# Modulation vectors moved between stages of a two-layer hybrid flow step

## The chip, the cores and the metric

The kernel runs on one core of a Trainium2 chip. The metric is the device time of one execution in microseconds; three runs of the kernel before gave 3373.78, 3359.71 and 3369.78 us, so the median is 3369.78 us. Engines are named as the profile names them: PE is TensorE, DVE VectorE, ACT ScalarE, POOL GpSimd; SP only issues transfers, and all transfers of this kernel go through its one queue, in order.

## The reference, cut to what matters

1152 tokens (1024 of a 64-column grid and 128 of context) of 1024 features pass two layers. In each layer six modulation vectors come from a conditioning vector, one set for the grid's condition and one for the context's:

```python
def ada_modulation(cond, w_mod, b_mod):
    m = (jax.nn.silu(cond) @ w_mod + b_mod)[..., None, :]
    return jnp.split(m, 6, axis=-1)

def trunk_layer(x, cond, p, ...):
    sh1, sc1, g1, sh2, sc2, g2 = ada_modulation(cond, p['w_mod'], p['b_mod'])
    h = rms_norm(x, p['norm1']) * (1 + sc1) + sh1
    xa, ga, bq, bff, bfb, bi, bg, cq, ck, cv = jnp.split(h @ p['w_in'], split_points, axis=-1)
    ... # three mixers: A RG-LRU, B HGRN2, C attention
    x = x + g1 * mix
    h2 = rms_norm(x, p['norm2']) * (1 + sc2) + sh2
    x = x + g2 * (jnp.square(jax.nn.relu(h2 @ p['w1'])) @ p['w2'])
```

The first two vectors are wanted at a layer's start, g1 at the output projection, sh2 and sc2 at the norm before the MLP, and g2 only in the MLP's second product.

## The kernel before, in words

Features lie on partitions. A vector of 1024 features is eight tiles of 128, so a layer has 48 modulation tiles, j = 0 to 47: 0 to 7 are sh1, 8 to 15 sc1, 16 to 23 g1, 24 to 31 sh2, 32 to 39 sc2, 40 to 47 g2. `mod_tile` (line 259) makes one tile for both conditions: it loads 128 rows of the transposed `w_mod`, 512 KB, in three pieces of 384, 384 and 256 columns (`wm`), and for each piece and condition runs one multiply-and-sum on VectorE against `sil`, the SiLU of the conditions spread over all partitions (`junk` is the product, `ma` the running sum, line 270). That is three transfers and six such VectorE instructions, each followed by a short read of the accumulator; a scale tile (sc1, sc2) has one more small VectorE instruction (`am`). Here each of the six is called a piece. Under the MLP and the attention the pieces' buffers come from the pool `sq` of four, under the recurrence of mixer A from `g`.

A layer's stages run one after the other, each woven from two or three streams: the recurrence of mixer A (RG-LRU) under projections; the recurrences of mixer B (HGRN2, a tree of levels, `sc` scores) under the other projections; the 36 query tiles of mixer C (`attention`), the first eight under the last projections, the others under the output projection (`wo`); the first product of the MLP, `w1`, and the second, `w2`. The MLP's products are done in blocks by seven products for eight; in the first there are 32 units (`line.add`), each of 84 matmuls, four outputs that VectorE and others take from PSUM (`hr`), and weights split into two parts on ScalarE, GpSimd and VectorE. The two layers run the same code on the same shapes.

Before, layer 0 makes its tiles 0 to 15 at its start, 16 to 47 under the recurrences (ten under A's, 22 under B's; `MODS`, line 457), and all 48 of layer 1 under its own first product, spread in program order over the units 6 to 31 (`MLP_MODS`). Layer 1 makes none; its `sil` is closed after that stage.

The order in which an engine runs its instructions is fixed when the program is built. The framework's scheduler takes the program and orders each engine's list by a simulated timeline; it may put an instruction well ahead of where the program wrote it, if its buffers allow. On the chip each engine, and SP's queue, runs its list strictly in order, waiting where something is not ready.

Of the kernel before, what the change touches and what calls it, by code (L numbers as in the profile page):

```python
# [15 lines left out]
DM = 1024  # L16
KD = DM // P
# [25 lines left out]
# a block of tokens: a quarter of the grid and one of the context  # L43
# [6 lines left out]
MLP_MODS = (6, 32)  # L50
# [9 lines left out]
def weave(main, n_main, side, n_side):  # L60
    """Emits two streams evenly interleaved, by their numbers of steps."""
    done = [0, 0]
    gens = [main, side]
    n = [max(n_main, 1), max(n_side, 1)]
    live = [True, True]
    while live[0] or live[1]:
        i = 0 if live[0] and (not live[1] or done[0] * n[1] <= done[1] * n[0]) else 1
        try:
            next(gens[i])
            done[i] += 1  # L70
        except StopIteration:
            live[i] = False


def weave_steps(main, n_main, side, n_side):
    """The main stream, with the steps of a side stream spread over its own."""
# [10 lines left out]
def weave_at(main, side, counts):  # L87
    """The main stream, with the given number of steps of a side stream after each of its own."""
# [10 lines left out]
def steps(n, span, i):  # L99
    """How many of n steps fall on i when they are spread over a span."""  # L100
# [17 lines left out]
def build(ctx, tc, I, O):  # L118
# [9 lines left out]
    def urgent(gen, offset):  # L128
        """A stream whose instructions go before those around it."""
# [7 lines left out]
    # pools that come and go  # L137
# [20 lines left out]
    def phase(st, tag, bufs, w=NW, side="left"):  # L158
        """A pool of [128, w] tiles for one phase of a layer."""
# [3 lines left out]
    def two_phases(st, tag, n1, n2, w):  # L163
        """The same in two places, by turns n1 and n2 tiles."""
# [66 lines left out]
    def load_cond(c):  # L231
        dma(sil[:, c], I["cond"][c:c + 1].to_broadcast([P, DM]))
        act(sil[:, c], sil[:, c], AF.Silu)
# [3 lines left out]
    # the early columns apart from the others, which come later  # L237
# [18 lines left out]
    # adaLN vectors, feature on partitions: mod[l][:, j, cond]  # L256
# [3 lines left out]
    def mod_tile(l, j, piece):  # L260
        """mod[l][:, j] from the rows of w_mod's transpose, in pieces."""
# [19 lines left out]
    def segs(n):  # L281
        # (lo, hi, cond) within chunk n
# [4 lines left out]
    def rms_sums(xs, n, alone=False):  # L287
        """The sums over the feature tiles of the squares of chunk n."""
# [14 lines left out]
    def rms_scale(sq, ps, w=P):  # L303
        """1/rms of 3w tokens, to be turned."""
# [11 lines left out]
    def rms_turn(R, ps, w=P):  # L316
        """1/rms of 3w tokens on all partitions, in SBUF."""
# [16 lines left out]
    class HT:  # L334
        """Normalised and modulated activations in two float32r parts, [k][n]."""
# [49 lines left out]
    def weight(src):  # L385
        """The float32r parts of a [128, 8, 128] weight tile, as functions of its k."""
# [17 lines left out]
    def project_tokens(l, group, ht, evac, s_):  # L404
        """256 features projected with the tokens on partitions, 128 tokens a step."""
# [16 lines left out]
    def store_mix(t, dst, n, g_):  # L422
        """The float32r parts of a chunk of 128 features of the mixers' output, to DRAM."""
# [7 lines left out]
    class B:  # L431
        """The arrays of one pair of heads, in chunks of 384 tokens."""
# [23 lines left out]
    # where the first layer's later modulation vectors are computed, of 32  # L456
    MODS = (10, 11, 11, 0)
    # the projections under the recurrences of the heads
# [5 lines left out]
    class HGRN:  # L464
        """The recurrence of one pair of heads.

        levels(g): the scores of chunk g's three blocks of 128 tokens, by the levels of a binary tree;
        tail(g): its state updates, and all but the backward states' part of its output;
        back(): the backward states, their part of the output and its norm, in reversed order.
        """  # L470
# [205 lines left out]
    def hgrns(pairs):  # L676
        """Both pairs of heads: the end of each part runs under the levels of the next."""
# [10 lines left out]
    RG_STEPS = 1 + 2 * 7  # L688

    def rglru(l, i, xa, gel, gw, ud, g_):  # L690
# [13 lines left out]
        # each function of ScalarE for both directions at once  # L704
# [53 lines left out]
    def split_q(ps, n, h_t, l_t, sub):  # L758
        # queries in the order (row half, column block, row, column) and scaled
# [20 lines left out]
    def qk_project(l, p, win, ht, qd, kd, s_, ns=range(NCH)):  # L780
# [9 lines left out]
        def evac_k(n, ps):  # L790
            # the grid's rows in pairs, by columns
# [12 lines left out]
    # the grid's upper half for all pairs of heads, then the context's tokens and the lower half  # L804
# [4 lines left out]
    # where the output projection is done, by the tokens' half: of the first features, of the last  # L809
# [3 lines left out]
    def attention(l, qd, kd, vd, pool, out):  # L813
        """All query tiles of the four pairs of heads.

        Yields once the first pair's operands are under way, then after each tile the one that is complete.
        """
# [169 lines left out]
    class Ends:  # L987
        """What becomes of the fifth product and of the four blocks of a product of blocks."""
# [4 lines left out]
    def lo_subs(n):  # L993
        """The engines of a version's seven subtractions, n of them on VectorE."""
        return iter([vsub if (i + 1) * n // 7 > i * n // 7 else psub for i in range(7)])

    class Weights:
        """The left operands of the seven products, version by version, in the order of their use."""
# [56 lines left out]
    class Line:  # L1055
        """Products of blocks one after the other, the end of each under the start of the next."""
# [53 lines left out]
    def pieces(b):  # L1110
        """Block b of tokens by chunks and conditions: (chunk, from, to, condition, place in the block)."""
# [795 lines left out]
```

## Time and profile before

| what | us |
|---|---|
| median of three runs | 3369.78 |
| lowest and highest run | 3359.71, 3373.78 |
| span of the profiled execution | 3359.0 |
| PE busy | 2987.9 (89%) |
| DVE busy | 2627.3 (78%) |
| POOL busy | 1735.7 (52%) |
| ACT busy | 1535.1 (46%) |

The profiled execution has no device time of its own beside its span. The median of the runs is 10.8 us above the span, and the lowest run 0.7 us. The shares are averages over stages with different limits, so the rows below are read stage by stage.

### The profile page before, as it was taken

The numbers are of one execution on the slowest core, as the hardware profiler recorded it, in microseconds if no ns is written. First come the engines' busy times: TensorE is split into PE (matmuls) and PEld (weight loads), VectorE is DVE, ScalarE is ACT, GpSimd is POOL, SyncE is SP. The second block draws the span as 40 slices with busy tenths as digits, with TensorE's granted clock in tenths as the row PEclk, the third lists the DMA queues.
The fourth block names the chain that finished last, engine by engine and source line by source line (L and its number), as shares of the span: only waits on it lengthen the run. The fifth ranks groups of instructions, "written<-read, shape, count | busy, mean of one in ns | idle before, by whom it ended". The sixth has DMA issues, their size and how long they took to land. (4 is left out here: it accounts for less than half of the span.)

```text
span 3359.0 us, 62376 instructions
## 1 busy us (share of the span) xinstructions
PE 2987.9 (89%) x21196; PEld 2829.2 (84%) x21196; DVE 2627.3 (78%) x6417; ACT 1535.1 (46%) x3878; POOL 1735.7 (52%) x1822
## 2 busy tenths in 40 slices
PE   7888998898788888898878899999988999899885
PEld 7877987797788888898878789988878999888885
DVE  7799964678999998999996687345878324899997
ACT  5453234554432225554555533455635333555445
POOL 4541222444744437777765311334546555777776
PEclk8999999999899989999999999999989999999997
DMA  7332449973355555322232212689644333532222
GB/s 269 83 115 89 135 117 272 262 244 114 116 164 159 154 163 171 96 85 89 73 117 67 57 31 78 185 245 289 193 130 122 109 105 106 166 98 86 89 73 73
DMA packets 391070, 452.26 MB, mean 135 GB/s; under 512 B 68192, under 2 KB 293600, under 8 KB 390752
## 3 DMA queue, kind: packets, MB, share of 16 engines
q1 hardware_dynamic: 390752, 448.28, 44.5%
q8 instruction: 168, 2.75, 0.3%
q14 instruction: 150, 1.23, 0.1%
HBM read 339.34 MB, written 108.79 MB: 133 GB/s over the span
## 5 line engine op out<-in xcount | busy, mean ns | idle before, releaser
L184 POOL TENSOR_TENSOR wl<-wr,wh 128x512 fp32r<-128x512 f32 x164 | 226.8, 1388 | 476.6 <-ACT wh L181 380.2
L184 POOL TENSOR_TENSOR ws<-wl,ws 128x512 fp32r<-128x512 f32 x160 | 230.6, 1445 | 231.6 <-ACT ws L181 223.5
L1081 PE MATMUL bB<-t,ws 128*128 128x288 f32 x768 | 240.6, 313 | 73.0 <-DVE hr L193 68.3
L1081 PE MATMUL bB<-T,wt 128*128 128x288 f32 x768 | 240.8, 314 | 67.7 <-ACT bB L181 51.0
L184 POOL TENSOR_TENSOR wt<-wl,wt 128x256 fp32r<-128x256 f32 x296 | 253.0, 862 | 68.7 <-ACT wt L181 65.3
L392 PE MATMUL pj<-hh,wh 128*128 128x384 f32 x640 | 221.5, 351 | 21.4 <-DVE vb L178 7.3
L1082 PE MATMUL bB<-t,ws 128*128 128x288 f32 x768 | 236.3, 308 | 1.0 <-DVE t L187 1.0
L1083 PE MATMUL bB<-t,ws 128*128 128x288 f32 x768 | 236.6, 308 | 0.0
L270 DVE CUSTOM_DVE_ANT_0 junk<-wm,sil,ma 128x384 bf16<-128x384 f32 (+1 forms) x320 | 230.0, 719 | 6.7 <-DMA wm<-in_w_mod 1.9
L1082 PE MATMUL bB<-T,wt 128*128 128x288 f32 x768 | 233.9, 305 | 0.0
L1083 PE MATMUL bB<-T,wt 128*128 128x288 f32 x768 | 232.9, 303 | 0.0
L394 PE MATMUL pj<-hh,wl 128*128 128x384 f32 x640 | 222.4, 348 | 4.2 <-POOL wl L184 4.2
L393 PE MATMUL pj<-hh,wh 128*128 128x384 f32 x640 | 222.9, 349 | 3.4 <-DVE hh L205 3.4
L1081 PEld LDWEIGHTS bB<-t,ws 128*128 128x128 f32 x768 | 153.5, 200 | 81.1 <-DVE hr L193 74.8
L1081 PEld LDWEIGHTS bB<-T,wt 128*128 128x128 f32 x768 | 150.5, 196 | 82.0 <-ACT bB L181 60.6
L184 POOL TENSOR_TENSOR wt<-wr,wt 128x256 fp32r<-128x256 f32 x210 | 184.4, 881 | 60.8 <-ACT wt L181 52.2
L184 POOL TENSOR_TENSOR T<-xb,T 128x288 fp32r<-128x288 f32 x192 | 180.6, 950 | 42.7 <-ACT T L181 42.1
L187 DVE TENSOR_TENSOR xb<-xb 128x288 f32<-128x288 f32 x288 | 190.8, 667 | 11.5 <-POOL B L184 6.3
L181 ACT CAST ws<-wl 128x512 fp32r<-128x512 f32 x160 | 98.7, 620 | 194.8 <-PE bB L1083 91.2
L181 ACT CAST T<-xb 128x288 fp32r<-128x288 f32 x256 | 110.3, 432 | 165.8 <-DVE xb L187 147.3
L1081 PE MATMUL bA<-B,wt 128*128 128x288 f32 x512 | 158.6, 310 | 26.7 <-DVE x L205 23.7
L205 DVE SCALAR_TENSOR_TENSOR x<-bB,mod,x 128x256 f32<-128x256 f32 (+2 forms) x576 | 169.7, 339 | 12.5 <-PE bB L1083 11.5
(336 smaller groups left out, 11474.7 us busy)
## 6 DMA issues: line engine op xcount, KB each, us to landing
wr<-in_w SPq DMA_DIRECT2D x308, 256.0 KB, 3.0
hd<-hr SPq DMA_DIRECT2D x256, 144.0 KB, 2.6
wm<-in_w_mod SPq DMA_DIRECT2D x160, 192.0 KB, 2.7
wr<-in_w_in SPq DMA_DIRECT2D x104, 256.0 KB, 3.1
bi<-in_bias SPq DMA_DIRECT2D x96, 192.0 KB, 4.3
QS<-qd SPq DMA_DIRECT2D x72, 256.0 KB, 4.2
xb<-hd SPq DMA_DIRECT2D x128, 144.0 KB, 2.2
xb<-hd SPq DMA_DIRECT2D x64, 288.0 KB, 2.8
```

The lines of the kernel that those rows point to most:

```text
L181: nc.scalar.copy(out=out, in_=in_)
L184: nc.gpsimd.tensor_tensor(out=out, in0=a, in1=b, op=ALU.subtract)
L187: nc.vector.tensor_tensor(out=out, in0=a, in1=b, op=ALU.subtract)
L205: nc.vector.scalar_tensor_tensor(out=out, in0=a, scalar=s, in1=b, op0=op0, op1=op1)
L270: nc.vector.tensor_tensor_reduce(out=junk[:, :w], in0=r[:, :w], in1=sil[:, c, k0:k0 + w], scale=1.0, scalar=acc[c], op0=ALU.mult, op1=ALU. ...
L392: mm(ps, lhsT=wh(k), rhs=ah(k), start=k == first, stop=False)
L393: mm(ps, lhsT=wh(k), rhs=al(k), start=False, stop=False)
L394: mm(ps, lhsT=wl(k), rhs=ah(k), start=False, stop=k == last)
L1081: mm(ps, lhsT=w[:, 0, ti(i)], rhs=t[:, 0], start=start and i == 0, stop=False, skip_group_check=True)
L1082: mm(ps, lhsT=w[:, 0, ti(i)], rhs=t[:, 1], start=False, stop=False, skip_group_check=True)
L1083: mm(ps, lhsT=w[:, 1, ti(i)], rhs=t[:, 0], start=False, stop=i == n - 1, skip_group_check=True)
```

## The change

The tiles stay the same, 96 in all, and so does what each one costs in instructions. Where they are computed changes:

| stage | before | after |
|---|---|---|
| layer 0, start | 16 | 16 |
| layer 0, recurrences of A and B | 32 | 24 |
| layer 0, first product of the MLP | 48 | 32 |
| layer 1, attention (query tiles 9 to 25) | 0 | 16 |
| layer 1, first product of the MLP | 0 | 8 |

Layer 0's first product now takes the layer's own g2 (40 to 47) and layer 1's 0 to 23. Layer 1's sh2 and sc2 (24 to 39) go under its attention, and its g2 (40 to 47) under its first product. For that `sil` is loaded and activated once more in layer 1, in memory that was kept empty as a pad.

```diff
-MLP_MODS = (6, 32)
+ATT_MODS, MLP_MODS = (9, 26), (6, 32)
...
-    MODS = (10, 11, 11, 0)
+    MODS = (8, 8, 8)
...
-        left = iter(range(16, 48 if l == 0 else 16))
+        left = iter(range(16, 40 if l == 0 else 16))
...
         if l:
-            # the same places as in the first layer
-            phase(h_st, "pad", 1, 2 * DM)("pad")
+            sil = phase(h_st, "sil1", 1, 2 * DM)("sil").rearrange("p (c d) -> p c d", c=2)
+            for c in range(2):
+                load_cond(c)
...
+        att_mods = iter([(l, 24 + 8 * i + k) for k in range(KD) for i in range(2)] if last else [])
+        mlp_mods = iter([(l, j) for j in range(40, 48)] + ([] if last else [(l + 1, j) for j in range(24)]))
+        n_mods = 8 if last else 32
...
             run_out(take(mid, MID.count(i)))
+            for a in take(att_mods, steps(16, ATT_MODS, i)):
+                mod_tile(*a, sqt)
...
-        later = iter(range(48))
...
-                elif not last:
-                    for _ in range(steps(48, MLP_MODS, n - 1)):
-                        mod_tile(l + 1, next(later), sqt)
+                else:
+                    for a in take(mlp_mods, steps(n_mods, MLP_MODS, n - 1)):
+                        mod_tile(*a, sqt)
```

What that does to the lists of instructions is seen on VectorE at three places. In the rows a line of the changed kernel is one higher than before (270 is 271); `ISA junk` is a piece, `ISA ma` or `ISA mod` the read of its sum.

The first place is the first product of layer 0, late in the stage. Between the third and the last output of a unit (`hr<-bB`, `hr<-bC`) VectorE had these rows before:

```order
L193 TENSOR_TENSOR hr<-bB,s_13313 128x288
L270 ISA junk,ma<-wm,sil,ma 128x384
L270 ISA ma 128x1
L205 SCALAR_TENSOR_TENSOR hr<-hr 128x288
L270 ISA junk,ma<-wm,sil,ma 128x384
L270 ISA ma 128x1
L187 TENSOR_TENSOR wl<-wl,wr 128x512
L270 ISA junk,mod_117<-wm,sil,ma 128x256
L270 ISA mod_117 128x1
L193 TENSOR_TENSOR hr<-bC,s_13313 128x288
```

and in the changed kernel, in the 22nd and 23rd unit:

```order
L193 TENSOR_TENSOR hr<-bB,s_13332 128x288
L205 SCALAR_TENSOR_TENSOR hr<-hr 128x288
L187 TENSOR_TENSOR wl<-wl,wr 128x512
L193 TENSOR_TENSOR hr<-bC,s_13332 128x288
L205 SCALAR_TENSOR_TENSOR hr<-hr 128x288
L187 TENSOR_TENSOR wl<-wr 128x512
L193 TENSOR_TENSOR hr<-bB,s_13468 128x288
L205 SCALAR_TENSOR_TENSOR hr<-hr 128x288
L193 TENSOR_TENSOR hr<-bC,s_13468 128x288
```

The scheduler doesn't thin the pieces out. It keeps the 12 to 14 pieces of each unit as they were up to the twentieth unit, and there the 192 pieces of 32 tiles are used up; before, the 288 pieces reached the 28th unit. Counted between one `hr<-bC` and the next, the fifth to the tenth unit have 8, 8, 9, 11, 12 and 13 pieces before, and 8, 8, 9, 10, 13 and 13 now.

The second place is the same stage of layer 1, in its fifth unit, where the operands of the second half of the tokens (`xb`, `t`) are made beside the weights. Before:

```order
L187 TENSOR_TENSOR wl<-wr,wl 128x512
L187 TENSOR_TENSOR t<-xb,t 128x288
L187 TENSOR_TENSOR ws<-wr,ws 128x512
L193 TENSOR_TENSOR wl<-wr 128x512
L187 TENSOR_TENSOR wl<-wl,wr 128x512
L187 TENSOR_TENSOR ws<-wr,ws 128x512
L187 TENSOR_TENSOR wl<-wr 128x512
L193 TENSOR_TENSOR hr<-bB,s_31315 128x288
L205 SCALAR_TENSOR_TENSOR hr<-hr 128x288
```

and now:

```order
L187 TENSOR_TENSOR wl<-wr,wl 128x512
L187 TENSOR_TENSOR t<-xb,t 128x576
L271 ISA junk,ma<-wm,sil,par_106 128x384
L271 ISA ma 128x1
L187 TENSOR_TENSOR t<-xb,t 128x288
L193 TENSOR_TENSOR wl<-wr 128x512
L187 TENSOR_TENSOR ws<-wr,ws 128x512
L187 TENSOR_TENSOR t<-xb,t 128x288
L271 ISA junk,ma<-wm,sil,ma 128x384
L271 ISA ma 128x1
L187 TENSOR_TENSOR wl<-wl,wr 128x512
L271 ISA junk,ma<-wm,sil,ma 128x384
```

The 48 pieces are not spread over the stage: counted in the same way, they stand in the fifth to the tenth unit, 7, 7, 9, 10, 13 and 2 of them, and none comes later.

The third place is the attention of layer 1 under the output projection: one query tile's maximum (`mx`), the local scores with their bias (`pl`), the output projection's sums (`x`) and the negated maximum (`nm`) that ScalarE's exponentials wait for. Before:

```order
L895 TENSOR_REDUCE mx<-sx 128x2
L923 RECIPROCAL rc<-rc 128x2
L187 TENSOR_TENSOR u<-av,u 128x2x4x16
L178 COPY ptl<-tl 128x384
L178 COPY ptc<-tc 128x256
L903 ISA pl,m_27460<-sl,bi,mx 128x384
L903 ISA m_27460 128x1
L903 ISA pl,m_27460<-sl,bi,mx 128x384
L903 ISA m_27460 128x1
L205 SCALAR_TENSOR_TENSOR x_26923<-wo,mod_117,x_26923 128x256
L205 SCALAR_TENSOR_TENSOR x_26923<-wo,mod_117,x_26923 128x32
L197 TENSOR_SCALAR nm<-m_27460 128x2
```

and now:

```order
L178 COPY ptc<-tc 128x256
L271 ISA junk,ma<-wm,sil,par_106 128x384
L271 ISA ma 128x1
L904 ISA pl,m_27244<-sl,bi,mx 128x384
L904 ISA m_27244 128x1
L904 ISA pl,m_27244<-sl,bi,mx 128x384
L904 ISA m_27244 128x1
L271 ISA junk,ma<-wm,sil,ma 128x384
L271 ISA ma 128x1
L205 SCALAR_TENSOR_TENSOR x_26537<-wo,mod_117,x_26537 128x256
L205 SCALAR_TENSOR_TENSOR x_26537<-wo,mod_117,x_26537 128x32
L197 TENSOR_SCALAR nm<-m_27244 128x2
```

Of the 96 pieces eight stand ahead of the tenth tile's maximum and 88 between the maxima of the thirteenth and the thirtieth tile, two to ten a tile, in front of rows that ScalarE, PE and GpSimd wait for.

In the recurrences the 48 pieces that go are about six ahead of the HGRN2 levels and about 42 at the end of their run, in the last eight levels that had pieces. In the list of PE, the first score of layer 0's attention now has 1154 of the projections' 1296 matmuls with features out (`pj`) before it, where it had 1235.

## Rows read from the trace of the kernel before

**Rows 1.** Windows by stage: busy us of each engine, granted clock, DMA share, GB/s.

```profile
core 0: us, PE busy (x) PEld busy (x) DVE busy (x) ACT busy (x) POOL busy (x), PEclk, DMA share, GB/s
120.80:799.60 678.80, 615.32 (x4579) 558.06 (x4578) 527.08 (x1531) 312.19 (x830) 235.89 (x286) 0.97 0.55 159
...
1813.50:2463.90 650.40, 611.66 (x4579) 555.83 (x4578) 404.78 (x1141) 314.21 (x831) 227.88 (x286) 0.98 0.50 142
...
799.60:1293.70 494.10, 419.65 (x2882) 410.72 (x2881) 456.86 (x959) 169.46 (x370) 254.40 (x202) 0.93 0.51 153
...
2463.90:2885.00 421.10, 398.00 (x2881) 393.25 (x2880) 228.07 (x366) 167.99 (x365) 236.73 (x200) 0.97 0.39 119
```

**Rows 2.** Waits of PE, first products: us in total, times, longest; layer 0, layer 1.

```profile
PE bB L1081 <- DVE hr L193: 53.1, 20, 4.8
...
PE bB L1081 <- DVE hr L193: 8.5, 3, 4.6
```

**Rows 3.** Windows of whole units in the first products, both layers.

```profile
908.20:982.40 74.20, 60.33 (x418) 58.67 (x419) 72.84 (x144) 26.31 (x57) 40.27 (x32) 0.95 0.50 156
982.40:1139.10 156.70, 135.39 (x929) 133.33 (x929) 153.81 (x360) 43.44 (x94) 76.30 (x61) 0.92 0.53 158
1139.10:1249.10 110.00, 94.00 (x652) 92.83 (x651) 108.18 (x258) 32.34 (x69) 48.36 (x40) 0.92 0.53 159
2569.60:2627.60 58.00, 54.09 (x386) 52.93 (x387) 42.82 (x49) 26.85 (x58) 38.31 (x31) 0.97 0.44 132
2627.60:2750.20 122.60, 122.60 (x926) 122.60 (x926) 35.10 (x68) 43.10 (x94) 67.22 (x61) 1.00 0.33 99
```

**Rows 4.** Line 270 alone in those of layer 0: us, DVE busy, clock, DMA.

```profile
908.20:982.40 74.20, 40.33 (x96) 0.95 0.50 156
982.40:1139.10 156.70, 112.16 (x284) 0.92 0.53 158
1139.10:1249.10 110.00, 73.13 (x194) 0.92 0.53 159
```

**Rows 5.** VectorE groups, one per unit: windows 982.4:1139.1, 1139.1:1249.1, 2627.6:2750.2.

```profile
L193 DVE TENSOR_TENSOR hr<-bC,s 128x288 f32<-128x288 f32 x12 | 5.4, 451 | 0.0
...
L193 DVE TENSOR_TENSOR hr<-bC,s 128x288 f32<-128x288 f32 x9 | 4.1, 450 | 0.0
...
L193 DVE TENSOR_TENSOR hr<-bC,s 128x288 f32<-128x288 f32 x12 | 5.5, 458 | 15.9 <-PE bC L1083 15.9
```

**Rows 6.** Windows inside the attention of layer 1.

```profile
2239.00:2281.00 42.00, 37.46 (x272) 31.44 (x273) 21.98 (x72) 21.15 (x69) 15.78 (x24) 0.92 0.98 283
2281.00:2389.00 108.00, 103.56 (x848) 92.31 (x849) 70.98 (x233) 60.80 (x201) 47.41 (x73) 0.98 0.96 285
```

**Rows 7.** VectorE group of one instruction per query tile, window 2281:2389.

```profile
L895 DVE TENSOR_REDUCE mx<-sx 128x2 f32<-128x512 f32 (+1 forms) x18 | 11.2, 622 | 0.0
```

**Rows 8.** All issues: transfers of the weights of the vectors.

```profile
wm<-in_w_mod SPq DMA_DIRECT2D x160, 192.0 KB, 2.7
wm<-in_w_mod SPq DMA_DIRECT2D x80, 128.0 KB, 2.4
```

**Rows 9.** The tile sil: its activation, and its transfers to landing; ScalarE table loads.

```profile
L208 ACT ACTIVATE sil<-sil x2: 1056/1059/1062, 10.5 to 53.8; 128x1024 f32<-128x1024 f32 x2
DMA to landing us min/median/max: 4.9/5.4/5.9
...
L208 ACT ACT_TABLE_LOAD x35 | 44.9, 1283 | 3.5 <-DVE nm L197 2.1 <-PEq L1897 0.7
```

**Rows 10.** Windows in the mixers of layer 0.

```profile
360.00:426.00 66.00, 64.03 (x506) 61.02 (x505) 64.31 (x197) 19.53 (x50) 15.96 (x16) 0.97 0.51 145
426.00:478.00 52.00, 47.48 (x372) 42.21 (x371) 41.62 (x122) 21.34 (x57) 14.75 (x16) 1.00 0.49 126
530.40:559.80 29.40, 21.30 (x131) 18.85 (x130) 12.33 (x33) 15.92 (x45) 9.66 (x12) 0.88 0.90 250
```

**Rows 11.** Waits of the DMA queue in the first product of layer 0.

```profile
SPq L211 <- DVE ma L270: 103.2, 82, 3.9
```

More of the change, by code (lines that the diff above doesn't have):

```diff
@@ L1302, in build @@
         kd = [tc.dram_tile([P, 2, T], F32, name=f"kd{l}{p}") for p in range(4)]
+        last = l + 1 == DEPTH
         xa = [[None] * NCH for _ in range(2)]
@@ L1610, in build @@
             run_out(take(mid, MID.count(i)))
+            for a in take(att_mods, steps(16, ATT_MODS, i)):
+                mod_tile(*a, sqt)
         ph2.close()
         x_st.close()
-        last = l + 1 == DEPTH
         hd = tc.dram_tile([NHID, P, T], F32, name=f"hd{l}")
```

## The prediction

> **What bounds the kernel now.** I read the busy time by stage first, then who PE waits for, then VectorE's groups, because the shares over the whole span mix stages with different limits. The two layers run the same code on the same shapes, and only layer 0 computes modulation tiles, so layer 1 shows what each stage of layer 0 would take without them. From the first gate of mixer A to the first matmul of the MLP layer 0 takes 678.8 us and layer 1 650.4; the first product of the MLP takes 494.1 and 421.1 us, with nearly the same matmuls and with VectorE busy for 456.9 and 228.1 us [rows 1]. So 32 tiles cost 28.4 us in the mixers and 48 cost 73.0 us in the first product. PE's waits say the same: for VectorE's outputs `hr` it waited 53.1 us in layer 0's first product and 8.5 us in layer 1's [rows 2].
>
> Inside the first product the pace of a unit is the thing to see. Between the first and the last of 12 `hr<-bC` lie 11 units, between those of 9 lie 8 [rows 5]. Layer 0 takes 156.7 / 11 = 14.25 us a unit and then 110.0 / 8 = 13.75, with VectorE busy 98% of the time; layer 1 takes 122.6 / 11 = 11.15 us, PE busy throughout and VectorE for 29% [rows 3]. The 284 and 194 rows of line 270 are pieces and reads by turns, so 142 pieces in 11 units and 97 in 8, 12 to 13 a unit [rows 4]. At that density VectorE is the limit; without pieces PE is.
>
> **First product of layer 0.** 96 of 288 pieces go, and a count of VectorE's work would give most of the 73 us back. The order says otherwise: the first twenty units keep the pieces that they had (142 in the same 11 units), and VectorE was the limit there, so their 14.25 us stay. Only the units 21 to 28 lose theirs, 97 pieces down to one. They took 110.0 us and will take PE's 8 x 11.15 = 89.2: a gain of 20.8 us, of which I count 20. Bounds: nothing, if something else holds those units, and 73.0 if the whole stage came to layer 1's length.
>
> **First product of layer 1.** It looks as if it could take eight tiles for nothing, since VectorE is idle for 46% of it [rows 1]. But the 48 pieces stand in the units 5 to 10, where the second half's operands are made. Layer 0 shows the price: five units with the very number of 48 pieces took 74.2 us there, and the same five units without pieces took 58.0 in layer 1 [rows 3, 4]. That is +16.2 us; I take +16. Bounds: 0 if they fit into gaps, and 48 x 0.84 = 40 if each adds what it lasts (40.33 us of 48 pieces with their reads [rows 4]).
>
> **Attention of layer 1.** Here 16 tiles come in, 88 of the 96 pieces between the maxima of the 13th and the 30th query tile; 18 maxima stand in that window of 108 us [rows 7]. In it VectorE is busy 70.98 us, PE 103.56, and the DMA engines 96% at 285 GB/s [rows 6]. Two prices for a piece can be read. By itself it lasts 0.84 us in the first product. But in the five units just used VectorE was busy for 72.84 us with 48 pieces and for 42.82 without [rows 3], so a piece added 0.63 us: the other instructions became shorter. I take 0.63, since that is what the stage paid for it. The Trainium skill has a reason in "SBUF — State Buffer", Who interferes with whom: an instruction of VectorE with two inputs in SBUF and one of GpSimd that reads SBUF shut each other out for a whole instruction. By that rule a GpSimd instruction holds up VectorE once, whatever stands in its way, which agrees; without it, at 0.84 a piece, VectorE's demand below would be 18 us larger. With 0.63, VectorE needs 70.98 + 88 x 0.63 = 126.4 us, and at the 98% that it reached in the first product 129, 21 us more than the window has. The transfers come to the same: 88 / 6 = 14.7 tiles of 512 KB [rows 8] are 7.7 MB, 27 us at 285 GB/s; with the 104 us that the engines were busy, 131 us, 23 more. These two overloads lie beside each other, so I count the larger, +23.
>
> The reload of `sil` comes before them, in a window with the DMA at 98% [rows 6]: two transfers of 512 KB, 5.4 us each to landing, then two activations of 1.06 us and two table loads of 1.28 on ScalarE [rows 9]. They stand in SP's queue ahead of the mixers' outputs (`u`) that the output projection waits for, and VectorE's first piece waits for them ahead of a `nm`. 1 MB at 283 GB/s is 3.7 us, and the other eight pieces fit there, VectorE being busy for half of the 42 us. I count +3. Bounds of the attention as a whole: +5 if the pieces fall into VectorE's waits and the queue runs ahead, and 96 x 0.84 = 81 plus 3 if they stand in the chain one by one.
>
> **Recurrences of layer 0.** Eight tiles go. In proportion that is 28.4 x 8 / 32 = 7.1 us. Most are the last pieces of the HGRN2 levels, and where they stood PE was busy 64.0 of 66.0 us with projections, so there it saves 2. Ending earlier, the levels let the attention begin with more projections left to put under it; what can be saved is PE's idle time behind them, 4.5 us in the next window and 8.1 us where the attention begins [rows 10]. The sum of these is 14.6. I take -9, with 0 and -28.4 as bounds.
>
> The second product keeps its order on every engine, and so do the start of layer 0 and layer 1's recurrences: nothing.
>
> **Sum.** -20 + 16 + 23 + 3 - 9 = +13 us on the span of 3359.0, that is 3372. The median of the runs shown stands 10.8 us above that span; carried over, it is 3383 us, 0.4% more than before. About 0.5%, 16.8 us, is what a measurement of this kernel can tell from no change.
>
> **Rivals.** First, the attention hides its tiles. For it: VectorE is idle 37 of the 108 us, and a tile's scores are made two tiles ahead of its output. Against it: transfers and VectorE are both over their time by the sum above, and the lists are fixed. It would leave +5 of the 26, and the time would be 3362. The Trainium skill argues for this side in "Perfetto Trace Analysis", Optimization Strategy: where the busiest engine changes between stretches of a kernel, interleaving them can help; here PE leads in the attention and VectorE in the first product, as the rows say, but the DMA is full where the work goes.
>
> Second, slower by more: SP's queue. Every `wm` transfer waits until VectorE has freed one of four buffers, and in the attention the loads of the next tiles' queries, values and bias stand behind it in the one queue. In layer 0's first product SP waited 103.2 us for `ma` alone [rows 11], 2.15 us a tile for 48. Sixteen tiles make 34 us; if the tiles' loads are late by that, on top of the transfers' 23 us, the attention costs 57 + 3 = 60 and the time is 3417. It decides from where the attention costs more than 30 us, for then the sum passes +17. Against it: the loads run two tiles ahead, about 12 us (108 / 17 x 2).
>
> Third, the first product of layer 0 gets faster throughout, because the scheduler's freedom or fewer transfers loosen the first twenty units too. A third of the tiles goes, so VectorE's line 270 loses 226 / 3 = 75 us, and with the stage at layer 1's length plus the 10 us of its early pieces the gain would be 60 instead of 20: 3343. (The 226 are the three windows' 225.6 [rows 4].) Against it stand the equal counts of pieces.
>
> **How the numbers follow.** My forecast has a chance of 0.50, and by itself the range 3366 to 3401: the attention 10 us either way, the three others some 5 each. The first rival has 0.24, spread from 3345 to 3368; the second 0.18, from 3395 to 3430; the third 0.08, from 3330 to 3352. Faster by over 0.5%, under 3352.9: all of the third and 0.06 of the first, 0.14. Slower by over 0.5%, above 3386.6: two fifths of my own case, 0.20, and the second, 0.38. The rest, 0.48, is within. The range for 8 times in 10 is 3348 to 3408: it leaves out about a tenth at each end.
>
> **What would show it.** In the profile of the changed kernel: units of layer 0's first product at 14 us up to the twentieth and at 11.2 behind it, the stage near 474 us; the fifth to ninth unit of layer 1 at 74 us instead of 58, the stage near 437; the 108 us of the attention near 130, VectorE over 95% busy in them and the DMA near full; the stretch from layer 0's first gate to its MLP near 670. I am wrong if the attention keeps its length, if layer 0's first product falls below 450 us, or if PE in the attention waits for loads (`QS`, `V`, `bi`) rather than for VectorE.

## The result, and the profile after

The changed kernel takes 3384.11 us (median of 6 runs, 3377.11 to 3393.42) against 3366.85 (median of 6, 3359.71 to 3373.78): 1.0051 times as long, 95% interval 1.0034 to 1.0068. The forecast was 3383, a little slower, and it came so; one term of its sum, a gain, did not come at all, and another was too large. The profiled run has a span of 3375.3 us, 16.3 more than before.

The windows of the same stages, after, in the order of [rows 1] (layer 0's mixers, layer 1's, then the two first products; the columns are those of [rows 1]):

```profile
core 0 of [0], span 3375.3 us
core 0: us, PE busy (x) PEld busy (x) DVE busy (x) ACT busy (x) POOL busy (x), PEclk, DMA share, GB/s
123.00:806.60 683.60, 621.56 (x4579) 563.88 (x4578) 500.25 (x1434) 312.52 (x831) 236.46 (x286) 0.97 0.54 151
1795.10:2471.50 676.40, 623.34 (x4579) 559.21 (x4578) 458.78 (x1341) 319.03 (x835) 235.41 (x286) 0.97 0.53 150
806.60:1276.60 470.00, 411.10 (x2882) 403.21 (x2880) 383.43 (x759) 169.69 (x370) 247.41 (x201) 0.95 0.48 142
2471.50:2902.80 431.30, 396.96 (x2882) 391.37 (x2880) 263.68 (x463) 169.69 (x370) 243.05 (x201) 0.97 0.43 126
```

Each stage against [rows 1]: layer 0's mixers +4.8 us, layer 1's +26.0, layer 0's first product -24.1. For layer 1's first product the window of before ends 1.5 us ahead of the second product's first matmul (2886.5), so it went from 422.6 to 431.3: +8.7. The sum is +15.4; the first gate starts 2.2 us later, and all other stages together give 1.3 back. A stage of one profiled execution has a scatter of its own: in the six kernels here whose lists of PE and VectorE are the same up to layer 0's MLP, its mixers last 678.8 to 682.8 us.

Inside the first products, whole units after, to be read beside [rows 3]: the eleven units with 13 pieces each in layer 0, the eight behind them, then layer 1's fifth to ninth unit, with 46 of its 48 pieces, and the next two:

```profile
988.78:1145.42 156.64, 133.94 (x918) 131.47 (x917) 153.75 (x362) 43.22 (x93) 73.53 (x59) 0.92 0.53 157
1145.42:1231.66 86.24, 86.24 (x652) 86.24 (x651) 33.38 (x60) 31.67 (x69) 44.17 (x40) 1.00 0.36 108
2576.52:2650.14 73.62, 60.87 (x420) 58.77 (x419) 73.05 (x141) 26.95 (x58) 40.88 (x32) 0.95 0.52 155
2650.14:2667.42 17.28, 17.28 (x132) 17.28 (x131) 9.86 (x18) 6.26 (x14) 10.15 (x9) 1.00 0.53 153
```

The prices of [rows 3] come back: 156.64 us for eleven full units (156.70 before), 73.62 for five units with 46 pieces (74.20 with 48 in layer 0 before). Behind such a run the units' outputs come closer together than 11.15 us for a moment: 17.28 us for two units. PE's own pace is the same (132 matmuls in 17.28 us are 131 ns each, 926 in 122.60 us of [rows 3] 132 ns); the other matmuls of these two units had run already, and VectorE's backlog is caught up there.

In the attention of layer 1, from the 13th query tile's maximum to the 30th, to be read beside the second row of [rows 6]:

```profile
2269.48:2403.29 133.81, 117.22 (x910) 101.29 (x909) 123.28 (x424) 61.25 (x202) 55.24 (x75) 0.96 0.99 296
```

It lasts 133.8 us, where 108 were read before, with VectorE busy 92% and the DMA engines 99%. VectorE's busy time there grew by 52.3 us over [rows 6], 0.59 for each of the 88 pieces.

### The profile page after: what moved, and what is told of

Its sections match the earlier page's. It is cut to its first block, busy times and chain, and to the rows that moved or that the text cites. A ratio compares the mean times of both kernels' runs of the same rounds, so it can differ in the third digit from the quotient of the medians.

```text
span 3375.3 us, 62367 instructions
## 1 busy us (share of the span) xinstructions
PE 2994.6 (89%) x21196; PEld 2828.2 (84%) x21196; DVE 2615.0 (77%) x6417; ACT 1540.9 (46%) x3883; POOL 1745.3 (52%) x1822
## 5 line engine op out<-in xcount | busy, mean ns | idle before, releaser
L1082 PE MATMUL bB<-t,ws 128*128 128x288 f32 x768 | 238.0, 310 | 64.5 <-DVE hr L193 62.2
L1083 PE MATMUL bB<-t,ws 128*128 128x288 f32 x768 | 234.3, 305 | 3.0 <-DVE t L187 3.0
L1084 PE MATMUL bB<-t,ws 128*128 128x288 f32 x768 | 233.9, 305 | 0.0
L202 POOL TENSOR_SCALAR pl<-pl,rc 128x384 f32<-128x384 f32 x128 | 82.3, 643 | 196.2 <-DVE rc L924 87.0
```

Of the source, the lines that this page charges most:

```text
L202: nc.gpsimd.tensor_scalar(out=out, in0=a, scalar1=s1, scalar2=s2, op0=op0, op1=op1)
L1082: mm(ps, lhsT=w[:, 0, ti(i)], rhs=t[:, 0], start=start and i == 0, stop=False, skip_group_check=True)
L1083: mm(ps, lhsT=w[:, 0, ti(i)], rhs=t[:, 1], start=False, stop=False, skip_group_check=True)
L1084: mm(ps, lhsT=w[:, 1, ti(i)], rhs=t[:, 0], start=False, stop=i == n - 1, skip_group_check=True)
```

## The experiments

The parts of the change one by one, on the kernel before. Times are medians; the ratio is to the runs of before beside them, with its 95% interval. The code is shortened to what matters. A "first gate" is the first matmul of mixer A's gates in a layer, a "maximum" a query tile's `mx`.

**Recurrences alone.** `MODS` as in the change, and tiles 40 to 47 of layer 0 nowhere:

```
-    MODS = (10, 11, 11, 0)
+    MODS = (8, 8, 8)
-        left = iter(range(16, 48 if l == 0 else 16))
+        left = iter(range(16, 40 if l == 0 else 16))
+        if l == 0: vcopy(mod[0][:, 40:48], mod[0][:, 16:24])
```

> The kernel before with one part of the change alone: eight tiles (40 to 47 of layer 0) are not computed under the recurrences; they are left out altogether and their values are a copy of other tiles. All else is as before. The forecast's step: layer 0 from the first gate of mixer A to the first matmul of the MLP 9 us shorter than the 678.8 of before, PE's idle time in it 9 less, and the time of the kernel about 3358. Rival, from the trace after: PE is busy for over 610 us of this stage in any case, so the pieces taken away free only VectorE; the stage stays between 676 and 686 and the time between 3363 and 3373. Second rival: what the change lost here it lost at the start of the attention, where the DMA engines were 95% busy; then tiles 5 to 6 take 18 us here too, and the stage is 683.

3368.74 us, ratio 1.0004 (0.9991 to 1.0018): nothing. The stage lasts 681.7 us, 2.9 more than before and inside the scatter of unchanged stages. First row: the whole stage; second: 40 us at the end of the HGRN2 levels.

```profile
core 0 of [0], span 3362.2 us
core 0: us, PE busy (x) PEld busy (x) DVE busy (x) ACT busy (x) POOL busy (x), PEclk, DMA share, GB/s
120.20:801.90 681.70, 624.99 (x4579) 567.43 (x4578) 500.30 (x1440) 312.57 (x831) 236.12 (x286) 0.96 0.54 152
440.20:480.20 40.00, 37.05 (x255) 32.10 (x252) 21.38 (x57) 13.11 (x35) 11.51 (x14) 0.91 0.24 70
```

The same 40 us, counted from the stage's first gate, in the kernel before:

```profile
440.80:480.80 40.00, 37.85 (x297) 34.32 (x294) 27.94 (x82) 15.84 (x42) 10.13 (x12) 1.00 0.39 104
```

PE's idle time did fall, from 63.5 us (678.80 - 615.32) to 56.7. But the same 4579 matmuls were busy for 9.7 us longer. At the end of the levels the granted clock was 0.91 where it had been 1.00, and one form of matmul through the stage (us busy, mean ns) took 361 ns where it had taken 349; this run, then before, where its line is one lower:

```profile
L393 PE MATMUL pj<-hm,wh 128*128 128x384 f32 x128 | 46.3, 361 | 7.5 <-DVE vb L178 4.5 <-ACT sg L208 3.0
```

```profile
L392 PE MATMUL pj<-hm,wh 128*128 128x384 f32 x128 | 44.6, 349 | 3.8 <-DVE vb L178 2.3 <-ACT sg L208 1.5
```

It is not one profile's luck. The changed kernel and the two made from it for its attention (below) have the same list of PE as this run up to layer 0's MLP; before and five of the runs below share the list with all 32 tiles. In the six with all tiles PE idles 63.5 to 70.9 us of the stage and is busy 610.8 to 615.8, and the 40 us have a granted clock of 1.00 each time. In the four without the eight it idles 56.7 to 62.0 us and is busy 620.6 to 625.0, with 0.87 to 0.91 in the 40 us.

**All 32 out, and 16 out.** `MODS = (0, 0, 0)` and `(6, 5, 5)`, the missing vectors copied.

> The same suspicion, four times as large: none of the 32 tiles under layer 0's recurrences is computed (their values are copies); the 48 tiles in layer 0's first product stay. If the tiles cost in proportion, as the forecast's step reckoned (28.4 us for 32, from the two layers' stages), the stage goes from 678.8 to about 650 and the kernel to about 3338. If PE's own work sets the stage, the stage can lose no more than the difference of PE's idle time between the layers (63.5 to 38.7 us) and is likely to lose far less, since PE waits there for gates of ScalarE and for loads too: stage 665 to 679, time 3352 to 3367.

3340.62 us, ratio 0.9924 (0.9908 to 0.9940); the stage 652.9 us, near the 650 of the proportion.

> The kernel before with 16 of the 32 tiles under layer 0's recurrences left out (their values are copies), between the runs with 8 (stage 681.7, 2.9 us longer than before) and with 32 left out (652.9, 25.9 shorter). If the cost is in proportion and the eight's result a matter of where PE happened to stall and its clock to fall, 16 give -13: stage 663 to 669, time 3350 to 3356. If there is a threshold (the first tiles taken away free only slack of VectorE, and only the later ones shorten the levels), 16 give -3 to +3: stage 676 to 682, time 3362 to 3369. In either case PE's idle time in the stage should be some 7 to 12 us below the 63.5 of before; what is lost against that stands in longer matmuls.

3353.70 us, ratio 0.9959 (0.9945 to 0.9974), so some 14 us; its profiled run, whose stage lasts 673.0 us, shows 5.8 of them. (The span of before lies 7.9 us under the median of its runs, this one's 0.1 above.) With 0, 8, 16 and 32 tiles out PE's idle time is 63.5, 56.7, 54.1 and 43.5 us, falling each time, and its busy time 615.3, 625.0, 618.9 and 609.4. By the times 16 and 32 tiles pay in proportion, and 8 do not: what they save in waits came back as longer matmuls. What makes the clock fall there was not isolated, and with 16 out the profiled run and the times differ, so the course between 8 and 16 stays open.

**First product of layer 0 alone.** The list there cut to 32 tiles:

```
-                        mod_tile(l + 1, next(later), sqt)     # 48 tiles
+        [(l + 1, j) for j in (*range(24), *range(40, 48))]   # 32 tiles
```

> The kernel before with another part alone: 16 tiles (24 to 39 of layer 1) are left out of layer 0's first product and their values are copies; the other 32 tiles keep their order. The forecast's step: the units up to the twentieth keep their 14.25 us, the later ones fall to 11.15, the stage is 20 to 25 us shorter than the 494.1 of before, and the time is 3342 to 3347. Rival: the stage gets faster throughout, because less is transferred and VectorE has a third less to do; it loses 60 us and the time is about 3307. Second rival: nothing, something else holds the late units; 3367.

3346.43 us, ratio 0.9935 (0.9917 to 0.9954). From the first product's start to layer 1's first gate it took 991.9 us instead of 1013.9: -22.0, inside the forecast's 20 to 25. "Faster throughout" falls.

**Attention of layer 1 alone.** The 16 tiles and the reload of `sil` are added, and the 48 tiles stay.

> The kernel before with the third part alone: layer 1's attention computes 16 tiles (24 to 39 of layer 1) once more, with sil loaded anew before it; the 48 tiles in layer 0's first product stay, so the same values are written twice. The forecast's step: the tiles stand in the attention at 0.63 us a piece over VectorE's and the DMA engines' time: 23 us and 3 for sil; from the 13th to the 30th query tile's maximum 130 us instead of 108, the time 3390 to 3395. Rival: the attention hides them in its waits and what the trace after shows there comes from the other parts (the order of the output projection, a later start): 5 us, the time about 3372. Rival of the queue: 60 us, 3427.

3394.54 us, ratio 1.0085 (1.0066 to 1.0103); layer 1's mixers last 678.9 us, +28.5. Not hidden, and not the queue's 60. From the 13th to the 30th maximum it takes 139.4 us, more than the 130 expected.

**Which of the two overloads?** Both on the changed kernel, in the attention only. Once the pieces read `sil` in place of a loaded tile; once the tiles are loaded and a piece takes 16 columns of them (both edits below, each for its own run):

```
-            r = piece("wm"); dma(r[:, :w], I["w_mod"][l, j][:, k0:k0 + w])
+            r = sil[:, 0, k0:k0 + w]                # no transfers
-            in0=r[:, :w], in1=sil[:, c, k0:k0 + w]
+            in0=r[:, :16], in1=sil[:, c, k0:k0 + 16]  # thin pieces
```

> The changed kernel, with the 96 pieces in layer 1's attention multiplying sil by itself: the same instructions of VectorE on the same shapes, and none of the 16 tiles' 512 KB loaded (the values of these 16 tiles are therefore others). From the attention's first scores to the MLP layer 1 took 295.7 us before and 320.2 after. The forecast's sum had two overloads of about the same size beside each other, VectorE's 21 us and the DMA engines' 23. If VectorE's is real, it stays without the transfers: 313 to 322 us for the stretch, time 3378 to 3386. If the transfers alone made the loss, the stretch falls to 296 to 302 and the time to 3360 to 3367. If each makes a part of it and they add, it is 306 to 312 and 3370 to 3377.

> The opposite of the run without transfers: the changed kernel with all 16 tiles loaded in layer 1's attention, but each of its 96 pieces, and all others of the kernel as they were, cut to the first 16 columns in this stage alone (the values of these 16 tiles are therefore others). VectorE's time for them falls from some 70 us to about 20. If the transfers made the loss, the stretch from the first scores to the MLP stays at 316 to 322 us and the time at 3380 to 3386. If VectorE made it, the stretch is 297 to 303 and the time 3361 to 3367. With both overloads real and side by side, as the forecast had them, this run too stays above 313.

Without transfers 3382.33 us (ratio to before 1.0034, 1.0021 to 1.0047), the stretch 314.4 us; thin pieces 3389.76 (1.0048, 1.0030 to 1.0067), the stretch 323.3. The first is in the range in which VectorE's overload is real, the second just above the one in which the transfers' is. Neither gives the whole loss back. From the 13th to the 30th maximum, without transfers:

```profile
2277.11:2398.75 121.64, 108.85 (x843) 94.38 (x842) 106.91 (x370) 60.43 (x200) 53.40 (x74) 0.93 0.82 244
```

and with thin pieces, then what VectorE waited for there (us in total, times, longest):

```profile
2276.97:2410.60 133.63, 114.08 (x863) 100.16 (x862) 96.73 (x420) 61.06 (x201) 48.90 (x74) 0.91 0.95 288
```

```profile
DVE junk L272 <- DMA wm<-in_w_mod: 21.5, 19, 2.7
```

The transfers alone keep the whole 26 us of this window: VectorE, with time to spare, stands 21.5 us behind pieces whose `wm` has not landed. VectorE's work alone, with the DMA at 0.82, keeps 13.7 of them. Over the whole stretch from the first scores to the MLP it keeps more, 18.7 of 24.5 us, since part of what the window gains is lost around it. They lie side by side, as the sum had them; the DMA's is the larger. In all five kernels that reload `sil` here (these two, the changed one, the run before and the next), 18.3 to 19.4 us pass from the 8th maximum to the 9th, where 9.7 passed before; in the changed kernel half of that is recovered by the 13th (46.61 us from the 8th, 41.67 before).

**The same tiles, spread.** The order fills VectorE: pieces are issued as early as it has room, 13 a unit, wherever the code asks for them. Here they may not pass the last `hr` of the unit before:

```
+                pace.append(vstt(t, t, 0.0, t, ALU.max, ALU.mult))
...
+                with tc.issue_after(pace[-1].ins):
                     nc.vector.tensor_tensor_reduce(out=junk[:, :w], ...
```

> The kernel before with the same 48 tiles in layer 0's first product, but spread: the pieces that follow a unit's call in the code may not be issued on VectorE before the last hr of the unit before it, so that units 7 to 32 get 10 to 12 pieces each and the earlier ones none, where before the units 5 to 28 got 8 to 14. The theory of the forecast is that a unit with 12 or 13 pieces takes 14.25 us since VectorE is full, one without takes 11.15, and one with fewer would fit into PE's time. VectorE needs 0.29 x 11.15 = 3.2 us for a unit's own work and 11 x 0.73 = 8.0 for the pieces: 11.3, about PE's 11.15. Then the stage loses 25 to 45 us of 494, and the time is 3320 to 3342. Rival: VectorE's total is what counts (456.9 us of 494 busy), spread or not; then the gain is under 10 us. Second rival: pieces in every unit delay hr each time, and the units cost 12.5 us or more: no gain or a loss.

3375.91 us, ratio 1.0015 (1.0001 to 1.0029): no gain. The theory fell: eleven late units with 10 and 12 pieces by turns took 144.48 us, 13.1 a unit, and VectorE was full. It was busy for 12.8 us a unit, so a piece took 0.87 beyond the unit's own 3.2, where the theory had 0.73.

```profile
1059.60:1204.08 144.48, 130.53 (x931) 128.65 (x931) 140.79 (x319) 43.22 (x93) 70.28 (x57) 0.96 0.54 159
```

The stage itself came to 482.9 us, 11.2 less, but up to layer 1's first gate nothing was left of that (1014.0 us, 1013.9 before); where it went was not looked into. This kernel also kept the reload of `sil` in layer 1, with no tile there to use it. That shows the reload's price: from the first scores to the MLP layer 1 took 299.4 us, and 294.5 to 298.6 in the nine kernels that have neither reload nor tiles there.

**Spread, and eight of layer 1's tiles in its own late units.** Layer 0's vectors where they were before, 40 tiles in layer 0's first product, no tile in the attention:

```
+    layer 0: [(l + 1, j) for j in range(40)], units 9 to 32
+    layer 1: [(l, j) for j in range(40, 48)], units 15 to 30, sil loaded in unit 11
```

> A version that computes all that the reference asks: layer 0's tiles where they were before (32 under the recurrences), 40 tiles of layer 1 spread over units 9 to 32 of layer 0's first product at 10 pieces a unit, and its tiles 40 to 47 over units 15 to 30 of layer 1's first product at 2 to 4 pieces a unit, with sil loaded during unit 11 there; none in the attention. By the forecast's prices layer 0's units fit into PE's time (3.2 + 10 x 0.73 = 10.5 of 11.15 us): the stage near 430 to 440 instead of 494, layer 1's first product 420 to 426 instead of 421, the attention as before: time 3300 to 3318. Rival, pieces delay hr wherever they stand: 12.5 us a unit, the stage near 455, layer 1's near 430, time 3330 to 3345.

3345.41 us, ratio 0.9922 (0.9904 to 0.9939). First row: twelve units of layer 0 with 10 pieces; second: fourteen of layer 1 with 2 to 4:

```profile
core 0 of [0], span 3335.4 us
core 0: us, PE busy (x) PEld busy (x) DVE busy (x) ACT busy (x) POOL busy (x), PEclk, DMA share, GB/s
1021.52:1171.76 150.24, 139.72 (x1016) 137.87 (x1015) 146.94 (x321) 47.33 (x102) 78.72 (x64) 0.98 0.55 161
2614.57:2770.55 155.98, 155.98 (x1178) 155.98 (x1177) 72.58 (x145) 57.96 (x122) 84.23 (x76) 1.00 0.42 125
```

Layer 1 computes its eight tiles for nothing (11.14 us a unit, and 894.1 us from its MLP to the end, 895.1 before), but ten pieces cost layer 0's units 12.5 us, as the rival had it. The pieces there (min/median/max in ns), and what ran on GpSimd beside them:

```profile
L274 DVE CUSTOM_DVE_ANT_0 junk<-wm,sil,par x40: 600/619/1730, 1027.7 to 1170.5; 128x384 bf16<-128x384 f32 x40
```

```profile
L184 POOL TENSOR_TENSOR ws<-wl,ws 128x512 fp32r<-128x512 f32 x24 | 34.2, 1424 | 34.7 <-ACT ws L181 34.6
...
L190 POOL TENSOR_TENSOR hr<-hr 128x288 f32<-128x288 f32 x24 | 21.6, 906 | 19.6 <-ACT hr L208 19.5
```

Half of these pieces take some 0.62 us; the longest takes 1.73, longer by a part of the 1.42 that one of GpSimd's subtractions lasts. In order of time (start, us), VectorE and then GpSimd:

```profile
1028.33 0.62 DVE L274 CUSTOM_DVE_ANT_0 junk<-wm,sil,par 128x384 bf16<-128x384 f32 x1
1028.99 1.52 DVE L274 CUSTOM_DVE_ANT_0 junk<-wm,sil,ma 128x384 bf16<-128x384 f32 x1
...
1028.54 1.56 POOL L184 TENSOR_TENSOR ws<-wl,ws 128x512 fp32r<-128x512 f32 x1 [0.81 <-ACT ws L181]
```

The first piece began before the subtraction and kept its 0.62 us; the second began during it and ended 0.41 us behind its end (1030.51, 1030.10). So it is throughout the window: the 41 pieces that met no GpSimd instruction took 0.60 to 0.62 us with 384 columns and 0.47 to 0.49 with 256, and each of the 49 longer ones (held pieces) ended 0.28 to 0.42 us behind the end of a GpSimd instruction. The other 30 kept their time: they began before the one that they met, or met only its last 0.06 us. All 120 pieces of the window by their shapes, 104.3 us together:

```profile
L274 DVE CUSTOM_DVE_ANT_0 junk<-wm,sil,ma 128x384 bf16<-128x384 f32 x40 | 38.5, 962 | 0.9
L274 DVE CUSTOM_DVE_ANT_0 junk<-wm,sil,par 128x384 bf16<-128x384 f32 x40 | 36.0, 900 | 0.9
L274 DVE CUSTOM_DVE_ANT_0 junk<-wm,sil,ma 128x256 bf16<-128x256 f32 x40 | 29.8, 744 | 1.1
```

**Less work on GpSimd.** One line more, in both first products:

```
                 act(t, ps, AF.Relu)
-                ptt(t, t, t, ALU.mult)
+                act(t, t, AF.Square)
```

> The paced version with one thing changed: in both first products the square of half of the hidden features (2 of 5.3 instructions a unit on GpSimd, 21.6 of the 79.3 us that GpSimd was busy in 150) is taken by ScalarE, which was busy for a third of the time. VectorE's and PE's instructions stay as they are. In the paced version a unit with 10 pieces took 12.5 us, VectorE being full, though 10 pieces at their median of 0.62 us and a unit's own 3.2 make 9.4. Theory: the missing 3 us are VectorE's instructions held up while one of GpSimd's runs (a piece took 0.62 in the median and up to 1.74 us); with 2 of 5.3 holds fewer, a unit takes 11.3 to 11.7, the stretch from the first product's start to layer 1's first gate falls from 984.7 to 960 to 968, and the time is 3318 to 3330. Rival: VectorE's time is its own or comes from its order and semaphores, GpSimd has no part in it; 12.5 us a unit, 3340 to 3347.

3313.64 us, ratio 0.9847 (0.9829 to 0.9864), the best of all, and nothing is left out. Twelve units of layer 0 with the same 10 pieces each:

```profile
1008.62:1150.66 142.04, 135.30 (x1009) 133.83 (x1009) 138.27 (x324) 57.40 (x125) 55.84 (x39) 1.00 0.58 170
```

GpSimd's busy time went from 78.72 to 55.84 us. VectorE got no fewer instructions, and its pieces took 93.1 us instead of 104.3, with 26 held ones instead of 49:

```profile
L274 DVE CUSTOM_DVE_ANT_0 junk<-wm,sil,ma 128x384 bf16<-128x384 f32 x40 | 36.2, 904 | 0.9
L274 DVE CUSTOM_DVE_ANT_0 junk<-wm,sil,par 128x384 bf16<-128x384 f32 x40 | 31.9, 796 | 0.9
L274 DVE CUSTOM_DVE_ANT_0 junk<-wm,sil,ma 128x256 bf16<-128x256 f32 x40 | 25.0, 626 | 1.1
```

A unit takes 11.84 us (142.04 / 12), a little over the 11.3 to 11.7 expected; the two profiled spans differ by 24.0 us. The Trainium skill has the mechanism in "SBUF — State Buffer", Who interferes with whom: a VectorE instruction with two inputs in SBUF and a GpSimd one that reads SBUF exclude each other for a whole instruction. The trace agrees: 11.2 us of the pieces' time went with GpSimd's instructions, which are not VectorE's, and the held pieces end behind a GpSimd instruction.

**Eight tiles more into the recurrences.** `MODS = (13, 13, 14)`, 32 tiles left in layer 0's first product; without and with the square on ScalarE.

> The paced version with eight tiles (0 to 7 of layer 1) taken from layer 0's first product to its recurrences, which then hold 40 tiles; 32 are left in the first product, 8 pieces a unit or 6. By the units measured so far (13 pieces 14.25, 11 pieces 13.2, 10 pieces 12.5 us, none 11.15) a piece costs 0.58 us over some 7.7 a unit and nothing below. Eight a unit: 11.2 to 11.5 us, 23 units gain 23 to 30; in the recurrences a tile cost 0.8 us by the run with all 32 left out (25.9 us): +6. Time 3320 to 3330. Rival: the cost is even from the first piece on (1.35 us for 10): 12.2 us a unit, a gain of 7 that the recurrences eat; 3342 to 3348. Second rival: as the run with eight left out there gained nothing, eight more cost nothing there; 3314 to 3322.

> Both together: eight tiles more in the recurrences, 8 pieces a unit in layer 0's first product, and half of the squares on ScalarE. If GpSimd's holds set the point from which a piece costs, the units are now PE's own: 11.15 to 11.2 us, 3 to 6 us below the run with eight tiles moved alone, time 3314 to 3326. If not, this run equals that one.

3343.64 us (ratio 0.9926, 0.9909 to 0.9944) and 3317.96 (0.9849, 0.9827 to 0.9872): no gain over the two kernels they start from. The first time is in the range of the rival with an even cost, but not for its reason: the first product did as expected (11.5 us a unit; with both, thirteen units in 144.87 us, 11.14 each), but layer 0's mixers took 705.3 and 710.2 us, where 681.6 and 682.8 were seen without the eight: 3.0 and 3.4 us a tile (the last from a profiled run whose span is 8.6 us over the median of its kernel's runs), not the 0.8 that I had divided out of the run with all 32 out. The stage without the eight (the kernel with pieces in late units), then with them:

```profile
122.53:804.15 681.62, 610.75 (x4579) 553.09 (x4577) 528.42 (x1529) 311.87 (x830) 237.37 (x286) 0.97 0.56 158
124.11:829.38 705.27, 625.63 (x4578) 561.38 (x4577) 557.97 (x1625) 313.61 (x831) 235.84 (x286) 0.96 0.57 159
```

PE idles 8.8 us longer there, some 1 us a tile, and is busy 14.9 us longer with the same matmuls: here too the larger part lies in PE's busy time. Why it grows is open.

## Why the prediction was right, and where it was not

**First product of layer 0, -20.** Right in mechanism: eleven full units up to the twentieth took the same time to 0.1 us. It came to -24.1. The eight later units took 86.24 us, 3.0 less than the 89.2 reckoned at 11.15 each, because the backlog is caught up behind the run. The run of this part alone gave -22.0.

**First product of layer 1, +16.** The mechanism holds (73.62 us where the step said 74.2), but the stage grew by 8.7, and by 10.5 and 12.0 in the two kernels made from the changed one for its attention, which have the same code here. The term was mis-sized: it stopped at the end of the five units. The next two took 17.28 us instead of 22.3, so 5 us came back at once. The cost lay in where and how densely the pieces stood, which no run takes apart: the same 48 pieces at 2 to 4 a late unit cost nothing.

**Attention of layer 1, +26.** The mixers grew by 26.0, and by 28.5 with this part alone. The window of 108 us came to 133.8, where 131 was said. Two overloads side by side is what the two runs that take one away showed. The 0.63 a piece came to 0.59. Inside the term, `sil` cost more than 3 at its place (9.6) and gave most back; the kernel that reloads it for nothing took some 3 us more over the stretch than the others. The first rival (hidden) falls by the run of this part alone. For the second (the queue), the DMA queue's waits in this window for VectorE's `ma` are 2.4 us, and the attention stayed under the 30 from which it decides:

```profile
SPq L211 <- DVE ma L271: 2.4, 4, 1.4
...
PE sx L880 <- DMA QS<-qd: 1.4, 1, 1.4
```

The second line answers one of the signs of being wrong: PE waited 1.4 us for queries there, out of 16.6 idle, and for the most part on VectorE, ScalarE and GpSimd. VectorE stayed at 92%, where over 95 was said.

**Recurrences of layer 0, -9.** This is the step that failed: "what can be saved is PE's idle time behind them". The idle time did fall, by 6.8 us in the run of this part alone and 1.4 in the changed kernel. It fell where the step said: the levels ended earlier (from the stage's first gate to layer 0's first attention score 401.0 us in the run alone, 409.6 before), the attention got more projections under it, and in the 29.4 us from that score PE idled 2.9 us instead of the 8.1 of [rows 10], with the DMA engines 98% busy instead of 90:

```profile
521.16:550.56 29.40, 26.49 (x164) 25.25 (x164) 12.98 (x38) 15.64 (x47) 9.37 (x14) 0.94 0.98 273
```

But the same matmuls took 9.7 and 6.2 us longer, and the stage was 2.9 and 4.8 longer instead of 9 shorter. I had taken PE's busy time as fixed. The four profiles without the eight tiles last 681.0 to 684.6 us and the six with them 678.8 to 682.8, so what is shown is that nothing was saved, not that the stage got slower. The lower clock at the end of the levels goes with it each time; why the clock falls there stays open.

**The sum.** It was +13 and came to +16.3: the errors of the last step (+14) and of layer 1's first product (-7) and layer 0's (-4) lie against each other. The forecast also carried 10.8 us from the span to the median, and the changed kernel shows 8.8, so the span's miss of 3.3 shrank to 1 in the time; the medians moved by 17.3 us, not 13. That the total was met so closely is partly luck; the order of the stages was not.

## What to carry to other kernels

Price added work by the place where it will stand, not by an engine's idle share over a stage: the same 48 pieces cost some 9 to 12 us in six early units and nothing spread over sixteen late ones. Two engines that hold each other up make a price that depends on both: before adding to a full VectorE, look at what GpSimd does beside it, and at the spread between the median and the longest of one instruction. And PE's busy time is no constant to subtract from: here a wait taken away came back as longer matmuls, with a lower granted clock in part of the stage.

## What was not expected of the hardware

A piece got dearer as they got fewer: the same 128x384 instruction (`ma`) took 845 ns in the mean at 13 a unit in the kernel before, and 962 at 10 a unit when spread, so VectorE stayed full (146.94 of 150.24 us). The time beyond 0.615 and 0.485 us a piece, which the pieces that met no GpSimd instruction took, shows why: it is 2.7 us a unit with 13 pieces and 3.0 with 10, for much the same work on GpSimd, and 2.0 with 10 after the squares went to ScalarE. What GpSimd takes from a unit hardly depends on the number of pieces, so fewer of them share it.

By the full units, 14.25 us with 13 pieces, 13.1 with 11 and 12.5 with 10, a piece costs 0.58 us at the margin. Carried on, that line meets PE's 11.15 us at some 7.7 pieces; the run with that many took 11.5 us a unit (138.35 / 12), so pieces are not free from there on. With the squares on ScalarE as well they were: 11.14.
